# A hand-written order for four engines from the last output tiles to the feed-forward operands, with two inverse norms as powers on GpSimd

## The chip, the cores and the metric

The kernel runs on one core of a Trainium2 chip. Its engines are TensorE (PE; its weight loads are listed apart as PEld), VectorE (DVE), ScalarE (ACT), GpSimd (POOL) and SyncE (SP, which issues the DMAs). The metric is the device time of one execution in microseconds; before the change the median of three runs is 1396.63 us (1396.52 to 1396.65). What a measurement of this kernel can tell from no change is about 0.2%.

## What is computed

One decoder layer on 1024 tokens of width 1024, all in float32: a norm, one input projection, two mixers (sparse attention with 8 heads, and a gated linear recurrence), an output projection added to the residual x, a second norm, and a gated feed-forward of width 2816:

```python
def rms_norm(x, g):
    y = xf * lax.rsqrt(jnp.mean(xf * xf, axis=-1, keepdims=True) + RMS_EPS)
    return (y * g.astype(jnp.float32)).astype(x.dtype)
...
    mix = jnp.concatenate([o_nsa.astype(x.dtype), o_hgrn.astype(x.dtype)], axis=-1)
    x = x + mix @ w_out[l]
    h = rms_norm(x, norm_ffn[l])
    gate, up = jnp.split(h @ w_gate_up[l], 2, axis=-1)
    x = x + (jax.nn.silu(gate) * up) @ w_down[l]
```

The change lies between the last parts of `mix @ w_out` and the first products of `h @ w_gate_up`.

## The kernel before, in words

Every float32 product is made from two parts of each factor, a high part (rounded to the matmul's type fp32r) and the rest. `split` (L111, L112) makes them: ScalarE copies the high part, VectorE subtracts it from the source. `mm3` (L118 to L120) is three matmuls: high by high, high by low, low by high. So the third matmul of a product, in the order of L118, L119, L120 or as the roles fall, needs a part that VectorE wrote.

Tokens are cut into 8 tiles of 128 (t = 0 to 7). For each, attention ends in `out_tile` (24 matmuls in two halves n = 0, 1; VectorE adds each half to x1, L497). Ahead of half 0, `mix_parts` (L510, L511) splits the tile of mixer output. After half 1, `norm_stats` squares the row on ScalarE (L242), and `rsqrt` makes the inverse norm from the sum in 12 VectorE instructions on 128x1 (L125 to L131: three, and three rounds of three). Then for t < 7 ScalarE multiplies x1 by it (L745), and GpSimd by the gain (L746), and subtracts tile t-4 from the first half where t >= 4 (L748). For t = 7 VectorE does both multiplications in one instruction (L743) with a second copy of the gain, g_last, that a DMA brings.

The feed-forward products are made by a two-by-two scheme with seven products per block, in which sums of halves take the place of one product in eight. Its operands are transposed halves of x1 and sums of them: b11 and b21 (tiles 0 to 3), b22 and t1o (tiles 4 to 7), and t2o, t3o, t4o from three differences d per pair of tiles (t, t+4), which GpSimd makes (L987 to L989; the first of pair 3 on VectorE). `operand` (L721 to L728) makes one tile of one operand: four transposes on TensorE into a bank (L724), a copy to the high part on ScalarE (L727), and a subtraction to the low part on VectorE (L728). b11 is ready before the last output tiles. The weights of a product are split like any factor; for the first two column blocks f = 0, 1 the kernel makes two products ahead of the loop: `first[f]` (weights times b11, in banks ps_t) and a second one (weights times b21, L967 sums them). The split weights of `first` lie in the pool `at`; when the block of that pool ends, its memory goes to the pool `ff`, from which the d tiles and the weight pages `epage` come. Then the loop over 22 column blocks begins; its first product is `q = product(s1, t1o)`, whose s1 GpSimd makes from two weight pages (L972).

The order of instructions on each engine is set by a scheduler in the framework, from the code's order and its own costs, except inside blocks that ask for manual scheduling. An engine works through its list in order; an instruction that waits holds up all that stand behind it.

Of the kernel before, what the change touches and what calls it, by code (L numbers as in the profile page):

```python
# [18 lines left out]
P = 128  # L19
# [29 lines left out]
def hybrid_layer(ctx: ExitStack, tc: tile.TileContext, x, x_t, par, w_in, k_norm, pos_k, pos_v,  # L49
# [87 lines left out]
    V.tensor_copy(identb, ident)  # L137
    par_t = const.tile([P, 18], F32, name="par_t")
# [100 lines left out]
    def norm_stats(src, junk):  # L239
# [4 lines left out]
        return rs  # L244

# [484 lines left out]
    with tc.tile_pool(name="at", bufs=1) as at:  # L730
        g_bc = at.tile([P, D], F32, name="g_bc")
        nc.sync.dma_start(g_bc, norm_ffn[0:1, :].broadcast_to([P, D]))
        def nsa_out(t, n):
            if n == 0:
                mixed[t] = mix_parts(qtok[:, t].rearrange("p (c n) -> p c n", c=4))
            out_tile(w_t, t, n, *mixed[t], bank_f)
            if n == 1:
                nc.sync.dma_start(x1_d[t * P:(t + 1) * P, :], x1[:, t, :])
                rs2 = norm_stats(x1[:, t, :], rpage())
                if t == NT - 1:  # L740
                    g_last = rpage()
# [156 lines left out]
        for i, u in enumerate(units + [None]):  # L898
# [46 lines left out]
    single_banks()  # L945
    opA = big.tile([P, 2, 2, 4, 512], F32R, name="opA", tag="A2")
# [3 lines left out]
    b21, t2o, b22, t1o, t3o, t4o = (opA[:, 0], opA[:, 1], opB[:, 0], opB[:, 1], opC[:, 0], opC[:, 1])  # L950
# [3 lines left out]
    def gate_up_a(f):  # L954
# [7 lines left out]
        return a, first.pop(0) if first else product(a[0, 0], b11), product(a[0, 1], b21, o=acc() if f < 2 else None)  # L962
# [335 lines left out]
```

## Time and profile before

| | |
|---|---|
| median of three runs | 1396.63 us |
| profiled execution, own time | 1396.95 us |
| its span, first to last instruction | 1395.2 us |
| TensorE busy | 1366.1 us, 98% of the span |
| VectorE / ScalarE / GpSimd busy | 74% / 43% / 23% |
[...]

The profile is of one execution. Busy time is counted per engine; matmuls overlap in it, so that a row's duration (0.39 us for 128x512) is longer than the step to the next row's start (0.23 us). [...] The stretch of the change lies at about 735 to 790 us of the span.

### The profile page before, as it was taken

To read this page: it belongs to the slowest core of one execution; us is meant where nothing else is said; L and a number is where in the kernel's file an instruction comes from. 1 tells how busy PE (TensorE), PEld (TensorE's weight loads), DVE (VectorE), ACT (ScalarE), POOL (GpSimd) and SP (SyncE) were. 2 spreads that over 40 slices of the span, in tenths; PEclk is the share of its full clock that TensorE was granted. 3 is DMA by queue.
4 is the path that set the end of the run, shared out by engine and by line. 5 is a ranking of instruction groups with operands and counts; after the bars stand their busy time and mean duration, and the time that the engine had idled before them with its cause. 6 is when DMAs were issued, how large, how long until landed. Compare 5 with 4: busy or idle time off the path is not lost.

```text
span 1395.2 us, 19645 instructions
## 1 busy us (share of the span) xinstructions
PE 1366.1 (98%) x7092; PEld 1127.8 (81%) x7092; DVE 1034.3 (74%) x1937; ACT 596.7 (43%) x1153; POOL 322.2 (23%) x297
## 2 busy tenths in 40 slices
PE   9999999999999999999998999999999999999998
PEld 7888888989977777777776788888888888888887
DVE  5317888626688887888867888888888887578764
ACT  7323333323446666566664433333333333444432
POOL 0001111011035443344345533323323320000000
PEclk9999999999999999999999999999999999999999
DMA  8411110111220001000003233333233336998521
GB/s 326 128 46 31 31 31 29 54 31 46 76 106 1 1 1 61 31 16 16 31 17 106 70 112 99 113 114 113 92 113 98 114 98 234 335 327 317 180 94 53
DMA packets 108768, 135.71 MB, mean 97 GB/s; under 512 B 6112, under 2 KB 63872, under 8 KB 108672
## 3 DMA queue, kind: packets, MB, share of 16 engines
q1 hardware_dynamic: 108672, 134.46, 28.6%
q8 instruction: 56, 0.92, 0.3%
q14 instruction: 40, 0.33, 0.1%
HBM read 105.87 MB, written 28.57 MB: 96 GB/s over the span
## 4 chain that ended last, share of the span: by engine, by line
PE 85%; DVE 10%; ACT 2%; issue 1%; POOL 1%; DMA 0%; ACTq 0%; POOLq 0%; DVEq 0%
PE bank L118 9%; PE bank L119 9%; PE bank L120 9%; PE a L118 8%; PE a L120 8%; PE a L119 8%; PE ps_t L120 4%; PE ps_t L119 4%; PE ps_t L118 4%; PE ps_t L861 3%; PE a L865 2%; PE a L866 2%; PE ps_t L375 1%; PE ps_s L839 1%; DVE nm L847 1%
## 5 line engine op out<-in xcount | busy, mean ns | idle before, releaser
L111 ACT ACTIVATE wop<-rpage 128x512 fp32r<-128x512 f32 x132 | 82.7, 630 | 156.8 <-PE bank L120 70.6
L850 POOL TENSOR_SCALAR pbig<-pbig,den,gates 128x640 f32<-128x640 f32 (+7 forms) x128 | 104.0, 817 | 167.0 <-DVE den L849 147.0
L112 DVE TENSOR_TENSOR wop<-rpage,wop 128x512 fp32r<-128x512 f32 x132 | 101.4, 771 | 13.4 <-ACT wop L111 11.3
L864 DVE TENSOR_TENSOR ph<-ps_t,ph 128x512 fp32r<-128x512 f32 x126 | 84.4, 684 | 18.5 <-ACT ph L863 17.6
L863 ACT ACTIVATE ph<-ps_t 128x512 fp32r<-128x512 f32 x126 | 72.7, 595 | 49.6 <-PE ps_t L861 38.7
L861 PE MATMUL ps_t<-ident,pbig 128*128 128x128 f32 x504 | 78.7, 275 | 2.1 <-POOL pbig L850 2.1
L381 POOL TENSOR_TENSOR kp<-kp,fp 128x256 f32<-128x256 f32 x28 | 20.3, 726 | 231.8 <-PE bank L358 180.3
L861 PEld LDWEIGHTS ps_t<-ident,pbig 128*128 128x128 f32 x504 | 61.0, 141 | 11.9 <-POOL pbig L850 3.2
L112 DVE TENSOR_TENSOR wlo<-wraw,whi 128x1024 fp32r<-128x1024 f32 (+2 forms) x27 | 32.0, 1188 | 46.2 <-PE a L120 19.3
L848 ACT ACTIVATE pbig<-ps_s,nm 128x640 f32<-128x640 f32 (+3 forms) x64 | 55.9, 875 | 24.1 <-DVE nm L847 19.0
L118 PE MATMUL bank<-wop 128*128 128x512 f32 x165 | 64.2, 389 | 0.0
L119 PE MATMUL bank<-wop 128*128 128x512 f32 x165 | 64.2, 389 | 0.0
L120 PE MATMUL bank<-wop 128*128 128x512 f32 x165 | 64.2, 389 | 0.0
L1012 POOL TENSOR_TENSOR tmp<-tmp,rpage 128x512 f32<-128x512 f32 x21 | 31.2, 1488 | 139.2 <-DVE wop L112 139.2
L111 ACT ACTIVATE wop<-act_a 128x512 fp32r<-128x512 f32 x48 | 30.3, 631 | 73.8 <-PE bank L120 48.3
L847 DVE TENSOR_REDUCE nm<-ps_s 128x1 f32<-128x640 f32 (+3 forms) x64 | 58.1, 914 | 4.7 <-PE ps_s L842 3.0
L865 PE MATMUL a<-ph,kv 128*128 128x512 f32 x132 | 58.8, 446 | 2.3 <-ACT ph L863 1.6
L866 PE MATMUL a<-ph,kv 128*128 128x512 f32 x132 | 57.5, 435 | 2.9 <-DVE ph L864 2.4
L112 DVE TENSOR_TENSOR wop<-tmp,wop 128x512 fp32r<-128x512 f32 x42 | 43.7, 1039 | 20.6 <-ACT wop L111 19.7
L111 ACT ACTIVATE wop<-tmp 128x512 fp32r<-128x512 f32 x42 | 26.6, 634 | 70.1 <-POOL tmp L1012 37.5
L112 DVE TENSOR_TENSOR wop<-act_a,wop 128x512 fp32r<-128x512 f32 x48 | 33.2, 691 | 30.7 <-ACT wop L111 30.6
L118 PE MATMUL a<-whi,hT_h 128*128 128x256 f32 (+2 forms) x168 | 55.2, 328 | 0.0
(458 smaller groups left out, 4352.3 us busy)
## 6 DMA issues: line engine op xcount, KB each, us to landing
rpage<-in_w_gate_up_dram SPq DMA_DIRECT2D x86, 256.0 KB, 3.1
raws<-in_w_down_dram SPq DMA_DIRECT2D x35, 512.0 KB, 7.5
act_a<-act_d SPq DMA_DIRECT2D x12, 1024.0 KB, 6.1
act_d<-as SPq DMA_DIRECT2D x33, 256.0 KB, 2.2
act_e<-act_d SPq DMA_DIRECT2D x6, 1024.0 KB, 8.2
act_d<-tmp SPq DMA_DIRECT2D x22, 256.0 KB, 2.2
act_d<-th SPq DMA_DIRECT2D x22, 256.0 KB, 2.1
xn<-in_x_dram SPq DMA_DIRECT2D x8, 512.0 KB, 6.0
```

The lines of the kernel that those rows point to most:

```text
L111: A.activation(hi, src, AF.Copy)
L112: V.tensor_tensor(lo, src, hi.bitcast(F32), op=OP.subtract)
L118: PE.matmul(o, ah, bh, start=first, stop=False, skip_group_check=chained)
L119: PE.matmul(o, ah, bl, start=False, stop=False, skip_group_check=chained)
L120: PE.matmul(o, al, bh, start=False, stop=last, skip_group_check=chained)
L847: V.tensor_reduce(nm, sv, axis=AX.XY, op=OP.max, negate=True)
L850: G.tensor_scalar(pp, pp, den, gates[:, qb, h * 3 + 1 + b:h * 3 + 2 + b], op0=OP.mult, op1=OP.mult)
L861: PE.transpose(pt[:, r * P:(r + 1) * P], wts[r][:, c0:c0 + P], ident)
L863: A.activation(ph[:, 0], pt, AF.Copy)
L864: V.tensor_tensor(ph[:, 1], pt, ph[:, 0].bitcast(F32), op=OP.subtract)
L865: PE.matmul(o, vst[b][:, kb, g, :], ph[:, 0], start=b == 0 and kb == kb0, stop=False)
L866: PE.matmul(o, vst[b][:, kb, g, :], ph[:, 1], start=False, stop=False)
```

## The change

Two things are done.

First, for tiles 6 and 7 `norm_power` takes the place of `norm_stats`: ScalarE squares as before, VectorE does one 128x1 multiplication and addition (L253 of the changed kernel), and GpSimd raises the result to the power -0.5 (L256, 128x1, with a constant column mhalf). The 12 small VectorE instructions of each of the two norms go. For tile 7 the power is issued later, where the code says `power()`.

Second, a block of manual scheduling reaches from the first product to the last operands. In it TensorE, VectorE, ScalarE and GpSimd follow the code's order; SyncE's is still the scheduler's. The code is written in a new order: the product first[0], two tiles of b21, the output tile of t = 7 in two different banks, two tiles of b21, first[1]; then for each pair of tiles the operands and differences, with the second product of f = 1 after the operands of pair 0 and that of f = 0 after those of pair 1, where before both came beside the first pairs' operands. The split of the mixer output of tile 7 stands ahead of the out tile; d(3)'s parts are split between VectorE and GpSimd as before. The line numbers grow: L724 to L728 become L743 to L747, L743 becomes L1039, L746 and L748 become L766 and L768, L987 to L989 become L1025, L497 becomes L511, L510 and L511 become L524 and L525.

```diff
+    mhalf = const.tile([P, 1], F32, name="mhalf")
+    V.memset(mhalf, -0.5)
...
+    def norm_power(src, junk):
+
+        ss = small.tile([P, 1], F32, name="n_ss", tag="n_ss")
+        rs = small.tile([P, 1], F32, name="n_rs", tag="n_rs", bufs=NT)
+        A.activation(junk, src, AF.Square, accum_out=ss)
+        V.tensor_scalar(ss, ss, 1.0 / D, EPS, op0=OP.mult, op1=OP.add)
+
+        def power():
+            G.tensor_tensor(rs, ss, mhalf, op=OP.pow)
+            return rs
+        return power
...
-        first = [product(qtok[:, f], b11, at.tile([P, 2, 512], F32R, name="wop0", tag="q", bufs=3), ps_t())
-                 for f in range(2)]
-        for t in nq:
+        hand.enter_context(tc.manual_schedule(engines={mybir.EngineType.PE, mybir.EngineType.DVE,
+                                                       mybir.EngineType.Activation, mybir.EngineType.Pool}))
+        w_first = [at.tile([P, 2, 512], F32R, name="wop0", tag="q", bufs=3) for f in range(2)]
+        for f in range(2):
+            split(w_first[f][:, 0], w_first[f][:, 1], qtok[:, f])
+        for t in nq[:-2]:
             nsa_out(*t)
+        first = [times(w_first[0], b11, ps_t())]
+        mixed[NT - 1] = mix_parts(qtok[:, NT - 1].rearrange("p (c n) -> p c n", c=4))
+        single_banks()
+        opA = big.tile([P, 2, 2, 4, 512], F32R, name="opA", tag="A2")
+        b21, t2o = opA[:, 0], opA[:, 1]
+        for t in range(2):
+            operand(b21, x1[:, t, 512:1024], t, bank_s)
+        nsa_out(*nq[-2])
+        power = nsa_out(*nq[-1], bank_o)
+        for t in range(2, 4):
+            operand(b21, x1[:, t, 512:1024], t, bank_s)
+        first.append(times(w_first[1], b11, ps_t()))
     p12.close()
...
-    nxt = [gate_up_a(0), gate_up_a(1)]
-    for t in range(3):
-        pair_a(t)
-    for t in range(3):
-        pair_d(t)
-        pair_b(t)
-    s1s = [gate_up_s1(0, nxt[0][0])]
+    g_last = rpage()
+    nc.sync.dma_start(g_last, norm_ffn[0:1, :].broadcast_to([P, D]))
+    aw = [gate_up_load(0), gate_up_load(1)]
+    pair_a(0)
+    pair_d(0)
+    pair_d(1, (0, 1))
+    rs2 = power()
+    V.scalar_tensor_tensor(x1[:, NT - 1, :], x1[:, NT - 1, :], rs2, g_last, op0=OP.mult, op1=OP.mult)
+    pair_d(1, (2,))
+    pair_b(0)
+    second = {1: product(aw[1][0, 1], b21, o=acc())}
+    pair_a(1)
+    pair_d(2)
+    pair_b(1)
+    second[0] = product(aw[0][0, 1], b21, o=acc())
+    pair_a(2)
+    V.tensor_tensor(x1[:, 7, 0:512], x1[:, 7, 0:512], x1[:, 3, 0:512], op=OP.subtract)
+    pair_d(3, (0,))
+    pair_b(2)
+    pair_d(3, (1, 2))
+    s1s = [gate_up_s1(0, aw[0])]
     pair_a(3)
-    pair_d(3)
     pair_b(3)
+    hand.close()
```

On TensorE, before, from the last output half (a_7472) to the second products (a_7554 and a_7577, of opA); x and d are sources of transposes:

```order
L119 MATMUL a_7472<-wlo,rpage 128x512
L120 MATMUL a_7472<-whi,rpage 128x512
L724 MATMUL bank<-ident,x_3322 128x128 x32
L724 MATMUL bank<-ident,d_7635 128x128 x4
L724 MATMUL bank<-ident,d_7636 128x128 x4
L724 MATMUL bank<-ident,d_7637 128x128 x4
L724 MATMUL bank<-ident,d_7662 128x128 x4
L724 MATMUL bank<-ident,d_7663 128x128 x3
L118 MATMUL a_7554<-opA,wop 128x512
L119 MATMUL a_7554<-opA,wop 128x512
L118 MATMUL a_7577<-opA,wop 128x512
L119 MATMUL a_7577<-opA,wop 128x512
```

After, from the last matmuls of first[1] (ps_t) to the second product of f = 1 (a_7588), which is now preceded by the 20 transposes of pair 0 alone:

```order
L120 MATMUL ps_t<-b_6855,wop_7392 128x512
L118 MATMUL ps_t<-b_6855,wop_7392 128x512
L119 MATMUL ps_t<-b_6855,wop_7392 128x512
L120 MATMUL ps_t<-b_6855,wop_7392 128x512
L743 MATMUL bank<-ident,x_3324 128x128 x8
L743 MATMUL bank<-ident,d_7553 128x128 x4
L743 MATMUL bank<-ident,d_7555 128x128 x4
L743 MATMUL bank<-ident,d_7557 128x128 x4
L118 MATMUL a_7588<-opA,wop 128x512
L119 MATMUL a_7588<-opA,wop 128x512
L120 MATMUL a_7588<-opA,wop 128x512
L118 MATMUL a_7588<-opA,wop 128x512
```

The first products' last matmuls moved from ahead of the output half to behind it, and one pair's operands stand ahead of a second product where before there were several.

On GpSimd, before, from tile 6's gain (L746) to the weight sum s (L972):

```order
L746 TENSOR_TENSOR x_3322<-x_3322,g_bc 128x1024
L748 TENSOR_TENSOR x_3322<-x_3322 128x512
L987 TENSOR_TENSOR d_7635<-x_3322 128x512
L988 TENSOR_TENSOR d_7636<-d_7635,x_3322 128x512
L989 TENSOR_TENSOR d_7637<-x_3322,d_7635 128x512
L987 TENSOR_TENSOR d_7662<-x_3322 128x512
L988 TENSOR_TENSOR d_7663<-d_7662,x_3322 128x512
L989 TENSOR_TENSOR d_7664<-x_3322,d_7662 128x512
L987 TENSOR_TENSOR d_7689<-x_3322 128x512
L988 TENSOR_TENSOR d_7690<-d_7689,x_3322 128x512
L989 TENSOR_TENSOR d_7691<-x_3322,d_7689 128x512
L972 TENSOR_TENSOR s_7716<-rpage 128x512
```

After, from tile 5's gain (L766) through both powers (L256) to the differences; d_7553 to d_7557 are those of pair 0, d_7559 to d_7565 those of pair 1:

```order
L766 TENSOR_TENSOR x_3324<-x_3324,g_bc 128x1024
L768 TENSOR_TENSOR x_3324<-x_3324 128x512
L256 TENSOR_TENSOR n_rs<-n_ss,mhalf 128x1
L766 TENSOR_TENSOR x_3324<-x_3324,g_bc 128x1024
L768 TENSOR_TENSOR x_3324<-x_3324 128x512
L1025 TENSOR_TENSOR d_7553<-x_3324 128x512
L1025 TENSOR_TENSOR d_7555<-d_7553,x_3324 128x512
L1025 TENSOR_TENSOR d_7557<-x_3324,d_7553 128x512
L1025 TENSOR_TENSOR d_7559<-x_3324 128x512
L1025 TENSOR_TENSOR d_7561<-d_7559,x_3324 128x512
L256 TENSOR_TENSOR n_rs<-n_ss,mhalf 128x1
L1025 TENSOR_TENSOR d_7565<-x_3324,d_7559 128x512
```

The power of tile 7 stands behind five differences that stood behind no power before. Their tiles come from the pool that takes over the memory of `at`.

On VectorE, before, the end of tile 7's inverse norm (L129 to L131) and its multiplication (L743), between evictions of transposes (L728) and weight splits (L112):

```order
L728 TENSOR_TENSOR opB<-bank,opB 128x4x128
L129 TENSOR_TENSOR rs_t<-n_rs 128x1
L728 TENSOR_TENSOR opA<-bank,opA 128x4x128
L130 SCALAR_TENSOR_TENSOR rs_t<-rs_t,rs_v 128x1
L728 TENSOR_TENSOR opC<-bank,opC 128x4x128
L131 SCALAR_TENSOR_TENSOR n_rs<-rs_t,n_rs 128x1
L112 TENSOR_TENSOR wop<-rpage,wop 128x512
L743 SCALAR_TENSOR_TENSOR x_3322<-x_3322,n_rs,rpage 128x1024
L112 TENSOR_TENSOR wop<-epage,wop 128x512
L728 TENSOR_TENSOR opC<-bank,opC 128x4x128
L728 TENSOR_TENSOR opA<-bank,opA 128x4x128
```

After, from the output halves (L511) on, with the multiplication (L1039) ahead of most evictions:

```order
L511 TENSOR_TENSOR x_3324<-a_7456,x_3324 128x512
L511 TENSOR_TENSOR x_3324<-a_7470,x_3324 128x512
L253 TENSOR_SCALAR n_ss<-n_ss 128x1
L747 TENSOR_TENSOR opA<-bank,opA 128x4x128 x2
L747 TENSOR_TENSOR opB<-bank,opB 128x4x128 x2
L1039 SCALAR_TENSOR_TENSOR x_3324<-x_3324,n_rs,rpage 128x1024
L747 TENSOR_TENSOR opA<-bank,opA 128x4x128
L747 TENSOR_TENSOR opC<-bank,opC 128x4x128 x2
L112 TENSOR_TENSOR wop<-epage,wop 128x512
L747 TENSOR_TENSOR opB<-bank,opB 128x4x128 x2
L747 TENSOR_TENSOR opA<-bank,opA 128x4x128
L747 TENSOR_TENSOR opC<-bank,opC 128x4x128 x2
```

The multiplication moved ahead, the small instructions are gone, and the weight splits stand between groups of evictions.

## Rows read from the trace of the kernel before

**Rows 1.** Part 4 of the page: the chain that ended last, share of the span by engine:

```profile
PE 85%; DVE 10%; ACT 2%; issue 1%; POOL 1%; DMA 0%; ACTq 0%; POOLq 0%; DVEq 0%
```

**Rows 2.** Busy time of each engine (instructions) in stretches, granted clock PEclk, DMA share, GB/s:

```profile
749.00:762.00 13.00, 8.46 (x58) 6.11 (x57) 12.14 (x25) 9.53 (x18) 10.67 (x9) 1.00 0.56 161
762.00:774.00 12.00, 9.99 (x58) 7.65 (x58) 10.61 (x15) 5.16 (x11) 7.02 (x6) 1.00 0.15 44
...
786.00:800.00 14.00, 14.00 (x63) 11.58 (x63) 12.15 (x20) 3.70 (x6) 4.46 (x3) 1.00 0.27 83
```

**Rows 3.** TensorE timeline: start us, us, engine line op out<-in xcount:

```profile
739.28 0.39 PE L120 MATMUL ps_t<-b,wop 128*128 128x512 f32 x1
739.51 0.40 PE L118 MATMUL ps_t<-b,wop 128*128 128x512 f32 x1
...
745.07 1.03 PE L724 MATMUL bank<-ident,x 128*128 128x128 f32 x8
746.01 0.50 PE L118 MATMUL a<-whi,rpage 128*128 128x512 f32 x1
```

**Rows 4.** VectorE timeline, same columns; [idle before <-releaser]:

```profile
739.32 0.43 DVE L888 TENSOR_TENSOR qtok<-a,fold 64x256 f32<-64x256 f32 x1
...
739.85 0.42 DVE L510 CAST rpage<-qtok 128x512 fp32r<-128x512 f32 x1
...
746.39 1.29 DVE L728 TENSOR_TENSOR opA<-bank,opA 128x512 fp32r<-128x512 f32 x2 [0.44 <-ACT opA L727]
...
752.26 0.53 DVE L129 TENSOR_TENSOR rs_t<-n_rs 128x1 f32<-128x1 f32 x1
...
761.75 2.30 DVE L743 SCALAR_TENSOR_TENSOR x<-x,n_rs,rpage 128x1024 f32<-128x1024 f32 x1
...
768.98 0.68 DVE L728 TENSOR_TENSOR opA<-bank,opA 128x512 fp32r<-128x512 f32 x1
769.58 1.28 DVE L728 TENSOR_TENSOR opC<-bank,opC 128x512 fp32r<-128x512 f32 x2
...
772.05 0.68 DVE L728 TENSOR_TENSOR opA<-bank,opA 128x512 fp32r<-128x512 f32 x1
```

**Rows 5.** ScalarE timeline of the same stretch:

```profile
738.47 0.38 ACT L886 ACTIVATE fold<-a 64x256 f32<-64x256 f32 x1
741.35 1.15 ACT L745 ACTIVATE x<-x,n_rs 128x1024 f32<-128x1024 f32 x1 [2.49 <-DVE n_rs L131]
745.76 1.09 ACT L727 ACTIVATE opA<-bank 128x512 fp32r<-128x512 f32 x2 [3.26 <-PE bank L724]
```

**Rows 6.** GpSimd timeline of the same stretch:

```profile
742.57 2.41 POOL L746 TENSOR_TENSOR x<-x,g_bc 128x1024 f32<-128x1024 f32 x1 [16.73 <-ACT x L745]
745.06 1.28 POOL L748 TENSOR_TENSOR x<-x 128x512 f32<-128x512 f32 x1
746.29 1.30 POOL L987 TENSOR_TENSOR d<-x 128x512 f32<-128x512 f32 x1
...
761.29 1.69 POOL L973 TENSOR_TENSOR rpage<-rpage 128x512 f32<-128x512 f32 x1
```

**Rows 7.** GpSimd timeline, 780 to 785 us:

```profile
781.91 1.63 POOL L1015 TENSOR_TENSOR epage<-epage,tmp 128x512 f32<-128x512 f32 x1
```

**Rows 8.** VectorE timeline, 780 to 784 us:

```profile
782.53 1.55 DVE L112 TENSOR_TENSOR wop<-tmp,wop 128x512 fp32r<-128x512 f32 x1 [0.15 <-ACT wop L111]
```

**Rows 9.** TensorE timeline, 766 to 778 us:

```profile
773.68 0.48 PE L118 MATMUL bank<-opB,wop 128*128 128x512 f32 x1
...
774.23 0.39 PE L120 MATMUL bank<-opB,wop 128*128 128x512 f32 x1
```

**Rows 10.** Busy time and granted clock in four stretches around 424 us:

```profile
421.00:424.00 3.00, 1.35 (x10) 0.88 (x8) 2.18 (x7) 2.62 (x9) 3.00 (x5) 1.00 0.00 0
424.00:427.00 3.00, 3.00 (x15) 2.52 (x14) 2.96 (x10) 1.97 (x7) 1.93 (x4) 0.54 0.01 3
```

**Rows 11.** The same view, 751 to 757.8 us:

```profile
751.00:754.40 3.40, 1.86 (x12) 1.20 (x12) 3.16 (x8) 2.88 (x8) 2.93 (x3) 1.00 0.92 260
```

More of the change, by code (lines that the diff above doesn't have):

```diff
@@ L714, in product, with times @@
         split(w[:, 0], w[:, 1], src)
+        return times(w, op, o)
+    def times(w, op, o):
         for c in range(4):
@@ L961, in gate_up_a @@
                 gu_load(a[k, j], FS[f], j, k)
-        return a, first.pop(0) if first else product(a[0, 0], b11), product(a[0, 1], b21, o=acc() if f < 2 else None)
+        return a
+    def gate_up_a(f):
+        a = gate_up_load(f)
+        return a, product(a[0, 0], b11), product(a[0, 1], b21)
     def gate_up_sum(f, o1, o2):
@@ L979, in pair_a, with pair_d @@
         operand(b22, x1[:, t + 4, 512:1024], t, bank_s)
-        if t == 3:
-            V.tensor_tensor(x1[:, 7, 0:512], x1[:, 7, 0:512], x1[:, 3, 0:512], op=OP.subtract)
         operand(t1o, x1[:, t + 4, 0:512], t, bank_s)
-    def pair_d(t):
+    def pair_d(t, some=(0, 1, 2)):
         xa, xb = x1[:, t, :], x1[:, t + 4, :]
-        d = dif[t] = [ff.tile([P, 512], F32, name=f"d{i}", tag="d", bufs=6) for i in range(3)]
-        (G if t < 3 else V).tensor_tensor(d[0], xb[:, 512:1024], xb[:, 0:512], op=OP.subtract)
-        G.tensor_tensor(d[1], d[0], xa[:, 0:512], op=OP.subtract)
-        G.tensor_tensor(d[2], xa[:, 512:1024], d[0], op=OP.subtract)
+        for i in some:
+            d = ff.tile([P, 512], F32, name=f"d{i}", tag="d", bufs=6)
+            dif[t, i] = d
+            (G if t < 3 or i else V).tensor_tensor(d, *((xb[:, 512:1024], xb[:, 0:512]), (dif[t, 0], xa[:, 0:512]),
+                                                       (xa[:, 512:1024], dif[t, 0]))[i], op=OP.subtract)
     def pair_b(t):
         for i, op in enumerate((t2o, t3o, t4o)):
-            operand(op, dif[t][i], t, bank_s)
-    for t in range(4):
-        operand(b21, x1[:, t, 512:1024], t, bank_s)
-    nxt = [gate_up_a(0), gate_up_a(1)]
-    for t in range(3):
-        pair_a(t)
-    for t in range(3):
-        pair_d(t)
-        pair_b(t)
-    s1s = [gate_up_s1(0, nxt[0][0])]
+            operand(op, dif[t, i], t, bank_s)
+    g_last = rpage()
[4 more added lines that the diff above has]
+    pair_d(1, (0, 1))
+    rs2 = power()
+    V.scalar_tensor_tensor(x1[:, NT - 1, :], x1[:, NT - 1, :], rs2, g_last, op0=OP.mult, op1=OP.mult)
[12 more added lines that the diff above has]
+    s1s = [gate_up_s1(0, aw[0])]
     pair_a(3)
-    pair_d(3)
     pair_b(3)
+    hand.close()
+    nxt = [(aw[f], first[f], second[f]) for f in range(2)]
     tmp = big.tile([P, 16, 512], F32, name="tmp", tag="A1")
```

25 lines of the change are left out of this document (12 added, 13 removed).

## The prediction

> **What bounds the kernel now.** I read the page's chain first, then the busy times of the changed stretch by stage, then each engine's timeline there. By the chain TensorE sets 85% of the span and VectorE 10% [rows 1], so a change pays only where TensorE idles. In the stretch it idles in one place. From 749 to 774 us it is busy 18.45 of 25 us, while VectorE is busy 22.75 [rows 2]: the evictions of transposes pace it, one per 0.60 us (768.98 to 769.58, [rows 4]). Idle time there, 6.55 us, is all that any order of this stage can win. After it TensorE has no slack, 14.00 of 14.00 us [rows 2], so what is late when the loop's first product q starts (773.68, [rows 9]) stays late to the end.
>
> **Part 1, the powers.** VectorE loses twelve 128x1 instructions per tile. For tile 7, nine of them lie between 752.26 and 761.75 with nine 0.60 us instructions of other kinds [rows 4]: 9.49 - 5.40 = 4.1 us of VectorE's time, the bounding engine's. That is the gain on offer. In exchange GpSimd gets a 128x1 power twice. No row shows one. From its 128x1024 (2.41) and 128x512 (1.28) operations [rows 6] a zero-column one costs 1.28 - 1.13 = 0.15 us; a dear one may cost as much as a whole 1024-column one, 2.41. I take 0.3, near the small end, as only one column is worked on, and keep both ends.
>
> **Part 2, the order up to the end of first[1].** First[0] ends where the next product starts now, 739.51 [rows 3]. Eight transposes take 745.07 to 746.01, 0.94 us [rows 3]: 740.45. Then the output half wants the low part of the mixer tile at its third matmul, at about 740.9. VectorE ends the second fold at 739.32 + 0.43 and a cast of 0.42 [rows 4], so it could subtract (L525) from 740.2. But GpSimd's gain of tile 6 (2.41 us, [rows 6]) is ready at about 740.1: ScalarE's fold ends at 738.85 and its scaling takes 1.15 [rows 5], the first power having been done by then. When VectorE's two-input subtraction from SBUF meets a GpSimd operation the rows show it waiting: L112 at 782.53 lasted 1.55 [rows 8], where an undisturbed subtraction of its size takes 0.68 (768.98, [rows 4]), and ended at 784.08, 0.54 after GpSimd's operation did (781.91 + 1.63, [rows 7]). So L525 ends at 740.07 + 2.41 + 0.54 = 743.0, and TensorE's third matmul starts at 743.1: 2.2 us lost. If VectorE is first, GpSimd is late by about 0.4 and these 2.2 us are not lost.
>
> [...]
>
> From there: 22 matmuls at 0.23 (739.28 to 739.51, [rows 3]) make 748.2, eight transposes 749.1, first[1]'s 12 matmuls 751.9.
>
> **Part 3, the wait that is new.** The first difference of pair 0 takes memory that pool `at` gives back, and the last reader of that memory is first[1]. Before, both first products were over when GpSimd came to it; now first[1] ends at 751.9. So GpSimd, free after L766 and L768 at about 743.8, waits 8 us. Behind it stand four more differences and the power of tile 7: 752.0 + 5 x 1.28 [rows 6] + 0.3 = 758.7. Behind the power VectorE's multiplication L1039 waits, and GpSimd has the next difference running by then. The same pair cost 2.30 us before: L743 started 0.46 after L973 and ended 1.07 after it (761.75 + 2.30 against 761.29 + 1.69, [rows 4, 6]). So L1039 ends at 761.0. VectorE works in order; three evictions of pair 0 stand behind (1.8): 762.8, then the split L112 of the second product's weights, 0.68 and some 0.15 of handover: its third matmul starts at 763.6. In that time TensorE, which has finished pair 0's transposes by about 758, has nothing that it may do: 5.5 us idle. The saved 4.1 us fall into this wait and buy nothing.
>
> **Part 4, groups and products in turn.** After this TensorE and VectorE alternate. Ten matmuls left of the second product: 765.9. The first eviction ends no sooner than 1.32 us after its group's first transpose starts, its subtraction starting then (745.07 to 746.39, [rows 3, 4]): 767.2. Five evictions 3.0, split and handover 0.83: 771.1. Ten matmuls: 773.4. The last group: 1.32, ten evictions and two subtractions at 0.60, 7.2, and about 1.1 where VectorE waits for two extra copies on ScalarE (0.54 each by [rows 5]): 783.0. With the handover q starts at 783.2, against 773.68: 9.5 us late. Before, q's third matmul came 0.55 after its first, without a wait [rows 9]. Now its split stands behind the two sums of the first products on VectorE: 0.6 x 3 less two matmuls, 1.4; the next product's split is late by about 1.3 in the same way. Sum 12.2.
>
> **Part 5, the clock.** Where TensorE was busy 1.35 of 3.00 us, the next 3 us ran at a granted clock of 0.54, the lower level; where it was busy 1.86 of 3.40, nothing fell [rows 10, 11]. The waits of 743 (2.2 us), 758 to 763.6 and those of the groups leave such thin stretches two or three times. A low stretch of 3 us costs between nothing, if TensorE waits in it anyway, and 1.4 us (0.46 x 3); I take 2 in all, of 0 to 5.
>
> The sum is 12.2 + 2 = 14.2 on the profiled execution's 1396.95 us (span 1395.2), which is 0.3 above the median of the three runs: 1396.63 + 14.2 = 1410.8, rounded to 1411.
>
> **Rivals.**
>
> *The differences don't wait* (0.13). If the memory isn't the one I think, GpSimd has the power of tile 7 done at about 750.5, and L1039 waits for nothing but its turn: after first[1], 751.9 + 1.32 and two evictions, at 754.4. It ends at 755.5, three evictions 757.3, split 758.1, and the rest as above: 760.4, 765.5, 767.8, 777.4, q at 777.7, 4.0 late, and 2.7 more at q: 6.7, or 4.5 without the wait at 743. 1401 to 1404. For it: the order of the pools is the framework's. Against it: nothing in the trace, since before the first difference started right behind L748, at 746.29 [rows 6], when first[1] had long ended.
>
> *A dear power and a low clock* (0.11). At 2.41 us each, the first power is hidden behind GpSimd's 8 us of waiting, the second is not: 2.1 more. If the clock stays at its lower level from 752 to 783, the two times ten matmuls on the path take 0.2 us more each, 4 in all, the transposes ahead of each group's first eviction some 0.5 each: 5.5 in the place of 2. Together 12.2 + 2.1 + 5.5 = 19.8, 1416; without the 2.1, 1414. For it: no power is in the trace, and three waits follow one another. Against it: one column is worked on, and evictions set the groups' time at either level.
>
> [...]
>
> *VectorE's freed time reaches TensorE, faster* (0.05). This is decided at one point: is the power of tile 7 done before VectorE comes to L1039 at 754.4, that is, does GpSimd start the first difference by 754.4 - 0.3 - 6.4 = 747.7? If so and if TensorE's products cover the evictions between them, VectorE starts on its backlog at 748.8 and needs the 23.7 us of before (749.07 to 772.73, [rows 4]) less 4.1 and less 1.2 of L743's wait: 767.2, q at 768.2, 5.5 earlier: 1391. Against it: TensorE has ten matmuls and the 1.32 us between two groups in which VectorE has nothing to do, twice 3.6 us, which alone eats the gain.
>
> *No change* (0.05): half of the faster case with the groups' waits, within 0.2% (2.8 us, what a measurement of this kernel can tell), 1394 to 1399.
>
> **How the numbers follow.** The forecast has 0.66, with its own range of 1405 to 1416: the sum without the wait at 743 and without the clock is 1396.6 + 10 = 1406.6, with the wait and the clock's upper end 1414, and a power of 2.41 us adds 2.1. The range for 8 times in 10 reaches to the first rival below and half of the second above: 1401 to 1418. Faster by over 0.2%: 0.05. Within: 0.05. Slower: 0.66 + 0.13 + 0.11 = 0.90.
>
> **What would show it.** In the trace of the changed kernel: L1025's first instruction on GpSimd starts right behind the last matmul of first[1], at about 752, with an idle time of some 8 us before it; L1039 waits for the power L256, and VectorE idles about 4 us before it; TensorE idles 5 us before the second product's third matmul, released by L112; L525 lasts 2.5 instead of 0.7 us; q starts near 783; behind q the two kernels' instructions run at one distance. The stage's VectorE time without idling falls by 4 us. I am wrong if the first difference starts near 744, or if TensorE is busy more than 20 of the 25 us between 749 and 774.

## The result, and the profile after

The changed kernel takes 1413.47 us (median of four runs, 1412.47 to 1414.38), the kernel before 1396.64: a ratio of 1.0121, with an interval of 1.0101 to 1.0141. A fourth execution of the kernel before took 1502.94 us and is left out of the ratio. 1411 was forecast. The profiled execution took 1414.38 us, its span is 1412.6. The granted clock is the share of full speed that the profile gives TensorE in a stretch; its mean over the span is 0.990 here and 0.997 in the kernel before. The lowest value in any window read here is 0.50 (743 to 746 us, below); "the low clock" means that.

Executions do not reach the stage of the change at one time. The second fold of the last attention block (L888, now L908) starts at 739.32 in the trace of before [rows 4] and at 737.74 here, though no instruction was moved ahead of tile 6's norm (the last section says why). So **lateness** below is counted from that row to the span's end: 1412.6 - 737.74 against 1395.2 - 739.32, which is 19.0 us. 1.58 us added to a time of this trace gives the time on the axis of the prediction.

The three stretches of [rows 2], in the changed kernel (window, length, then busy time of TensorE, its weight loads, VectorE, ScalarE, GpSimd, then granted clock, DMA share, GB/s):

```profile
749.00:762.00 13.00, 7.17 (x37) 4.90 (x35) 5.75 (x9) 5.63 (x10) 9.68 (x8) 0.79 0.62 182
762.00:774.00 12.00, 8.31 (x32) 6.39 (x32) 5.79 (x10) 3.22 (x6) 3.48 (x3) 0.66 0.23 66
...
786.00:800.00 14.00, 11.81 (x40) 9.25 (x41) 12.41 (x16) 7.36 (x13) 8.25 (x7) 0.76 0.27 76
```

From 749 to 774 TensorE is busy 15.48 us instead of 18.45, at clocks of 0.79 and 0.66, and VectorE, which was busy 22.75, only 11.54: the stage is no longer paced by evictions, every engine waits. GpSimd's timeline, the counterpart of [rows 6]:

```profile
735.96 0.56 POOL L256 TENSOR_TENSOR n_rs<-n_ss,mhalf 128x1 f32<-128x1 f32 x1 [11.66 <-DVE n_ss L253]
738.53 2.36 POOL L766 TENSOR_TENSOR x<-x,g_bc 128x1024 f32<-128x1024 f32 x1 [2.00 <-ACT x L765]
...
752.17 1.27 POOL L1025 TENSOR_TENSOR d<-x 128x512 f32<-128x512 f32 x1 [9.59 <-DVE opA L747]
...
757.31 1.26 POOL L1025 TENSOR_TENSOR d<-d,x 128x512 f32<-128x512 f32 x1
758.53 0.56 POOL L256 TENSOR_TENSOR n_rs<-n_ss,mhalf 128x1 f32<-128x1 f32 x1
759.05 1.27 POOL L1025 TENSOR_TENSOR d<-x,d 128x512 f32<-128x512 f32 x1
760.28 2.25 POOL L1025 TENSOR_TENSOR d<-x 128x512 f32<-128x512 f32 x1
```

The first difference starts at 752.17, 0.25 us after TensorE went on from first[1], behind 9.59 us of idle time, and the power of tile 7 comes at 758.53, right behind the five differences that stand ahead of it on GpSimd, though VectorE wrote its input (L253) from 750.35 to 750.50. (The releaser named, an eviction on VectorE, is not the last one: that eviction ended at about 742.7. In the trace of e1, below, the releaser named is first[1] itself.) A power of 128x1 took 0.56 us, the first as the second. VectorE's timeline, the counterpart of [rows 4]:

```profile
738.66 2.77 DVE L525 TENSOR_TENSOR rpage<-qtok,rpage 128x512 fp32r<-128x512 f32 x1
...
759.12 2.28 DVE L1039 SCALAR_TENSOR_TENSOR x<-x,n_rs,rpage 128x1024 f32<-128x1024 f32 x1 [4.65 <-POOL n_rs L256]
...
763.12 1.30 DVE L112 TENSOR_TENSOR wop<-epage,wop 128x512 fp32r<-128x512 f32 x1
770.64 1.32 DVE L747 TENSOR_TENSOR opB<-bank,opB 128x512 fp32r<-128x512 f32 x2 [6.21 <-ACT opB L746]
```

L525 lasts 2.77 us beside GpSimd's L766; the multiplication L1039 waits 4.65 us for the power, and takes 2.28 us, as L743 did (2.30, [rows 4]); between the groups VectorE is idle 6.21 us. TensorE's timeline, the counterpart of [rows 3, 9]:

```profile
741.49 0.50 PE L120 MATMUL a<-whi,rpage 128*128 128x512 f32 x1 [2.05 <-DVE rpage L525]
...
751.69 0.39 PE L120 MATMUL ps_t<-b,wop 128*128 128x512 f32 x1
751.92 1.03 PE L743 MATMUL bank<-ident,x 128*128 128x128 f32 x8
...
759.76 0.80 PE L118 MATMUL a<-opA,wop 128*128 128x512 f32 x1 [3.02 <-ACT wop L111]
...
764.48 0.79 PE L120 MATMUL a<-opA,wop 128*128 128x512 f32 x1 [3.49 <-DVE wop L112]
765.07 0.63 PE L118 MATMUL a<-opA,wop 128*128 128x512 f32 x1
765.50 0.63 PE L119 MATMUL a<-opA,wop 128*128 128x512 f32 x1
...
786.55 0.50 PE L118 MATMUL bank<-opB,wop 128*128 128x512 f32 x1 [2.44 <-ACT wop L111]
...
788.92 0.80 PE L120 MATMUL bank<-opB,wop 128*128 128x512 f32 x1 [1.64 <-DVE wop L112]
```

The brackets give the length of a wait and what ended it. The clock between some of these rows, the same columns as above:

```profile
743.00:746.00 3.00, 3.00 (x8) 2.34 (x7) 0.69 (x1) 0.00 (x0) 0.00 (x0) 0.50 0.02 5
...
764.00:769.00 5.00, 4.52 (x11) 3.45 (x12) 0.42 (x1) 0.00 (x0) 1.56 (x1) 0.50 0.28 83
771.00:776.00 5.00, 3.43 (x18) 2.29 (x17) 3.34 (x6) 2.25 (x5) 0.00 (x0) 1.00 0.00 0
...
789.00:794.00 5.00, 5.00 (x12) 3.94 (x13) 4.85 (x6) 2.82 (x5) 3.22 (x2) 0.50 0.00 0
```

From 735 to 800 us TensorE's waits, by the view of waits, sum to 17.5 us; in the kernel before they sum to 6.4. The difference of 11.1 and the low clock on the path (6.2, worked out in "The size") make 17.3 of the 19.0; the rest is not assigned. At the low clock matmuls stepped by 0.43 us (765.07 to 765.50) instead of 0.23 ([rows 3]).

### The profile page after: what moved, and what is told of

It reads as the page before. It is cut to its first block, busy times and chain, and to the rows that moved or that the text cites. A ratio compares the mean times of both kernels' runs of the same rounds, so it can differ in the third digit from the quotient of the medians.

```text
span 1412.6 us, 19630 instructions
## 1 busy us (share of the span) xinstructions
PE 1372.4 (97%) x7092; PEld 1131.6 (80%) x7092; DVE 1035.5 (73%) x1916; ACT 597.3 (42%) x1153; POOL 324.9 (23%) x299
## 4 chain that ended last, share of the span: by engine, by line
PE 84%; DVE 10%; ACT 3%; issue 1%; POOL 1%; DMA 0%; ACTq 0%; POOLq 0%; DVEq 0%
PE bank L120 9%; PE bank L118 9%; PE bank L119 9%; PE a L120 8%; PE a L119 8%; PE a L118 8%; PE ps_t L118 4%; PE ps_t L119 4%; PE ps_t L120 4%; PE ps_t L881 3%; PE a L885 2%; PE a L886 2%; PE ps_t L389 1%; PE ps_s L859 1%; DVE nm L867 1%
## 5 line engine op out<-in xcount | busy, mean ns | idle before, releaser
L112 DVE TENSOR_TENSOR wop<-rpage,wop 128x512 fp32r<-128x512 f32 x132 | 102.4, 777 | 13.3 <-ACT wop L111 11.2
L112 DVE TENSOR_TENSOR wlo<-wraw,whi 128x1024 fp32r<-128x1024 f32 (+2 forms) x27 | 32.0, 1188 | 46.0 <-PE a L120 19.3
L112 DVE TENSOR_TENSOR wop<-act_a,wop 128x512 fp32r<-128x512 f32 x48 | 33.2, 691 | 33.8 <-ACT wop L111 33.7
L112 DVE TENSOR_TENSOR wop<-tmp,wop 128x512 fp32r<-128x512 f32 x42 | 42.7, 1018 | 18.6 <-ACT wop L111 18.0
```

Of the source, the lines that this page charges most:

```text
L112: V.tensor_tensor(lo, src, hi.bitcast(F32), op=OP.subtract)
```

## The experiments

Every run is compared with the kernel before on the same chip; "late" is the lateness defined above, from the run's profiled execution. It is one execution's, with that execution's low clock in it; what a run won or lost is read from the medians. The intervals of e1, e5 and e6 overlap that of the changed kernel, those of e3 and e7 just touch it, the others lie clear of it.

| run | median us | ratio to before (95%) | late us |
|---|---|---|---|
| changed kernel | 1413.47 | 1.0121 (1.0101 to 1.0141) | 19.0 |
| e1 power early | 1410.84 | 1.0104 (1.0089 to 1.0119) | 13.0 |
| e2 first[1] in front | 1407.56 | 1.0080 (1.0065 to 1.0095) | 12.3 |
| e3 by hand, no powers | 1408.95 | 1.0089 (1.0074 to 1.0104) | 13.1 |
| e4 powers alone | 1401.50 | 1.0034 (1.0024 to 1.0045) | 4.7 |
| e5 added matmuls | 1412.37 | 1.0112 (1.0098 to 1.0126) | 16.0 |
| e6 mix first | 1411.23 | 1.0104 (1.0090 to 1.0118) | 15.6 |
| e7 s early | 1409.36 | 1.0088 (1.0075 to 1.0102) | 12.5 |
| e8 reordered | 1397.44 | 1.0005 (0.9996 to 1.0014) | 1.3 |
| e9 e2 and e7 | 1404.96 | 1.0060 (1.0045 to 1.0075) | 8.6 |
| e10 no order by hand | 1402.78 | 1.0045 (1.0032 to 1.0059) | 5.4 |
| e11 multiplication first | 1396.69 | 1.0004 (0.9995 to 1.0013) | -0.5 |
| e12 e11 without powers | 1397.41 | 1.0006 (0.9997 to 1.0015) | 1.3 |

**e1, the power of tile 7 ahead of the differences.**

```diff
     pair_a(0)
+    rs2 = power()
     pair_d(0)
     pair_d(1, (0, 1))
-    rs2 = power()
```

> One move: the power of tile 7 stands on GpSimd ahead of the differences of pair 0 instead of behind five of them. Theory A (the power is late because it stands behind differences that wait for the memory of first[1], and VectorE's multiplication waits for it): the power is done near 751, the multiplication starts after two evictions of opB at about 754.5 instead of 759.1, and the second product's third matmul comes 3.5 to 4.5 us earlier, limited next by the split of its weight page, whose copy waits for a DMA that landed at 759.1; 1407 to 1410. Rival B (the alternation of groups and products sets the time, whatever the power does): not below 1412. Rival C (the two powers themselves are dear): no change.

Measured 2.6 us less than the changed kernel, 1410.84, just above theory A's range; the intervals of the two ratios overlap, so the mechanism is read from the trace. GpSimd, VectorE and ScalarE of e1:

```profile
752.84 1.27 POOL L1025 TENSOR_TENSOR d<-x 128x512 f32<-128x512 f32 x1 [1.02 <-PE ps_t L120]
```

```profile
755.46 2.30 DVE L1039 SCALAR_TENSOR_TENSOR x<-x,n_rs,rpage 128x1024 f32<-128x1024 f32 x1 [0.31 <-POOL d L1025]
...
760.49 1.51 DVE L112 TENSOR_TENSOR wop<-epage,wop 128x512 fp32r<-128x512 f32 x1 [0.94 <-ACT wop L111]
```

```profile
759.83 0.63 ACT L111 ACTIVATE wop<-epage 128x512 fp32r<-128x512 f32 x1 [1.81 <-DMA epage<-in_w_gate_up_dram]
```

The difference still waits, and what ends its wait is first[1] (ps_t). The multiplication no longer waits for a power, only 0.31 us until a difference is over. The next bound is as expected the split's copy, which waits for a DMA: the page's memory, too, comes from the pool that first[1] reads, and in the changed kernel its DMA is issued at 752.68, 0.76 us after TensorE went on from first[1] (751.92); in the kernel before, with first[1] in front, the first of the two was issued at 745.01. So the power's place was one wait of two; the other one has the same cause. The lateness in this trace fell by 6.0 us, more than the median: 1.6 of them are a low clock behind the wait for L525 that did not come here, though nothing was changed there (last section).

**e2, first[1] ahead of the output halves.**

```diff
-        first = [times(w_first[0], b11, ps_t())]
+        first = [times(w_first[f], b11, ps_t()) for f in range(2)]
...
-        first.append(times(w_first[1], b11, ps_t()))
```

> One move: the product first[1] stands on TensorE directly behind first[0], ahead of the output halves of tile 7, as in the kernel before; the rest of the order by hand stays. Theory A: its 12 matmuls fill the 2.05 us in which TensorE waits for L525, the differences and the weight pages no longer wait for it, the power of tile 7 is done when VectorE comes to it, and pair 0 starts 3.9 us earlier; second product's third matmul near 756.5 instead of 764.5; with less low clock 1403 to 1406. Rival B (groups and products in turn): only the 2 us of L525 are won, 1411 to 1412. Rival D (the memory wait is not first[1]'s): differences start at 752 again, 1411.

Measured 1407.56, 5.9 us less, above theory A's range and far from its rivals' 1411. GpSimd and VectorE:

```profile
742.90 1.29 POOL L1024 TENSOR_TENSOR d<-x 128x512 f32<-128x512 f32 x1
...
749.74 0.56 POOL L256 TENSOR_TENSOR n_rs<-n_ss,mhalf 128x1 f32<-128x1 f32 x1 [0.34 <-DVE n_ss L253]
```

```profile
753.90 1.30 DVE L1038 SCALAR_TENSOR_TENSOR x<-x,n_rs,rpage 128x1024 f32<-128x1024 f32 x1 [1.42 <-DMA rpage<-in_norm_ffn_dram]
```

The first difference starts at 742.90 instead of 752.17, without idle time, and the power at 749.74: what held both was first[1], as the prediction said. The gain fell short of the forecast. Its trace shows another wait, 1.42 us for the DMA of g_last, and the low clock, which was expected to shrink, in three places again (steps of 0.43 us at 758 to 760, 767 to 770 and 783 to 788); how much each of them cost is not shown.

**e3, the order by hand without the powers.**

```diff
-                if t < NT - 2:
-                    rs2 = norm_stats(x1[:, t, :], rpage())
-                else:
-                    power = norm_power(x1[:, t, :], rpage())
-                    if t == NT - 1:
-                        return power
-                    rs2 = power()
+                rs2 = norm_stats(x1[:, t, :], rpage())
+                if t == NT - 1:
+                    return rs2
```

> The order by hand stays, the two powers go back to twelve small VectorE instructions each. Theory A (what the power saved falls into a wait): VectorE makes tile 7's inverse norm itself by about 752.7, the multiplication waits for nothing at 755 to 756, so this kernel is faster than the changed one in spite of some 5 us more VectorE work: 1406 to 1411. Rival E (the power saves VectorE time that counts, and the order alone is the loss): 1415 to 1418.

1408.95, as theory A says: with more work on VectorE the kernel is 4.5 us faster than the changed one. In its trace tile 7's multiplication (L1034 there) starts at 755.10 without a wait, while the first difference still waits for first[1], until 751.31. Two things are mixed in it: tile 7's norm no longer waits for GpSimd, and tile 6's comes later, so that L525 meets no GpSimd operation (0.69 us in its trace), which e6 prices alone.

**e4, the powers alone**, in the kernel before with the scheduler's order.

```diff
-                rs2 = norm_stats(x1[:, t, :], rpage())
+                rs2 = (norm_stats if t < NT - 2 else norm_power)(x1[:, t, :], rpage())
```

> The kernel before with the two powers alone, all engines ordered by the scheduler. The nine to twelve small VectorE instructions go from a stage that VectorE paces, 4 us. Theory F (freed VectorE time reaches TensorE when no order by hand stands against it): 1392 to 1394. Theory G (the scheduler's list shifts with it, and what is won ahead of q is given back where q's split stands): 1395 to 1400. Rival C (powers are dear): above 1400.

1401.50, some 5 us slower than before: theory F is wrong, and the time lies above what G gave and in the range of C. The trace tells C from G. TensorE and VectorE around q:

```profile
773.72 0.50 PE L118 MATMUL bank<-opB,wop 128*128 128x512 f32 x1
...
777.64 0.50 PE L120 MATMUL bank<-opB,wop 128*128 128x512 f32 x1 [3.19 <-DVE wop L112]
...
781.64 0.50 PE L120 MATMUL bank<-opA,wop 128*128 128x512 f32 x1 [0.85 <-DVE wop L112]
```

```profile
775.71 1.28 DVE L979 TENSOR_TENSOR tmp<-a,tmp 128x512 f32<-128x512 f32 x2
776.90 0.68 DVE L112 TENSOR_TENSOR wop<-s,wop 128x512 fp32r<-128x512 f32 x1
```

The powers take 0.56 us here too, and tile 7's multiplication waits for a DMA (1.15 us), not for the power. q starts as late as before (34.1 us behind the second fold; before 773.68 - 739.32 = 34.4), but its third matmul waits 3.19 us for a split that the scheduler now puts behind two sums of the first products, and the next product 0.85. That is theory G with its size underrated: the time that was freed ahead of q was lost again at q.

**e5, matmuls added in two waits.**

```diff
+    def warm(n):
+        o = bank_s()
+        for i in range(n):
+            PE.matmul(o, b11[:, 0, 0, 0:P], b11[:, 0, 0], start=i == 0, stop=i == n - 1)
...
+    warm(30)
     second = {1: product(aw[1][0, 1], b21, o=acc())}
...
     pair_b(3)
+    warm(16)
     hand.close()
```

> The changed kernel, and in two of TensorE's waits matmuls that nobody reads: 30 of 128x512 ahead of the second product of f = 1 (from 756.7 to about 763.6, where the product's third matmul came at 764.5) and 16 ahead of q (783 to 786.7). They take no work away. Theory K (the low clock behind thin stretches costs on the path): matmuls at 764 to 769 and at 789 to 794 step 0.23 instead of 0.43 us, ten and some ten of them, 2.0 + 2.2 us less: 1408.5 to 1411. Rival (the clock falls in time that is waited anyway, or for another reason): within 1 us of the changed kernel, 1412.5 to 1414.5; if the added matmuls get in the way, later.

1412.37: 1.1 us less, between the two ranges; inconclusive by time. The clock in e5:

```profile
764.00:768.00 4.00, 4.00 (x23) 3.37 (x22) 0.24 (x1) 0.05 (x1) 1.40 (x1) 1.00 0.31 87
...
771.00:776.00 5.00, 4.41 (x11) 3.23 (x12) 1.27 (x3) 0.20 (x1) 0.00 (x0) 0.67 0.00 0
...
788.00:793.00 5.00, 3.63 (x14) 2.54 (x15) 4.85 (x6) 2.81 (x6) 3.29 (x2) 1.00 0.00 0
```

In both places the product ran at full clock (1.00 in the first and the third row), as theory K says; but now the clock fell to 0.67 at 771 to 776, over the other second product, which ran at full clock in the changed kernel (1.00 for the same window, above). The third low stretch, behind L525, is missing in e5 as well (1.00 from 744 to 747 us), though nothing was changed there. So the low clock can be taken away at one place and come at another; that it would go if the waits went is not shown by this run.

**e6, VectorE ahead of GpSimd at L525.** The scaling of tile 6 is issued after two operand tiles.

```diff
-                    rs2 = power()
-                A.activation(x1[:, t, :], x1[:, t, :], AF.Copy, scale=rs2)
...
+                    rs2 = power()
+                    if hand_on:
+                        return lambda: scale(t, rs2)
+                scale(t, rs2)
...
         for t in range(2):
             operand(b21, x1[:, t, 512:1024], t, bank_s)
+        scale6[-1]()
         nsa_out(*nq[-2])
```

> The changed kernel with ScalarE's scaling of tile 6, and GpSimd's two operations behind it, moved behind two evictions in the code, so that VectorE's L525 (738.7) starts ahead of GpSimd's L766 (then about 740.8). Theory L (L525 loses 2.05 us because GpSimd's operation started first): L525 lasts 0.7 us, TensorE's output half waits for nothing, and the low clock at 743 to 746 (1.4 us) goes with the wait; GpSimd's later end is hidden by its wait for first[1]. 2 to 3.5 us less: 1410 to 1411.5. Rival (L525 waits for something else, or GpSimd's delay counts): no change, 1413 to 1414.5.

1411.23, 2.2 us less, in theory L's range. L525 in e6:

```profile
738.66 0.69 DVE L525 TENSOR_TENSOR rpage<-qtok,rpage 128x512 fp32r<-128x512 f32 x1
```

It starts at the same 738.66 and takes 0.69 us instead of 2.77. By time alone e6 and the changed kernel overlap; the row does not. In e6 GpSimd's operation starts only at 740.82, when L525 is over, so this run prices the meeting and does not show who wins one. The changed kernel's rows show both orders: L525, 0.13 us behind L766, lasts until 0.5 us after it; and the difference that GpSimd starts at 760.28, while VectorE's L1039 runs, takes 2.25 us instead of 1.27. The kernel before has the second order too: L973, which started at 761.29, 0.15 us behind L112 on VectorE, took 1.69 us [rows 6], where L987, on operands of the same size, took 1.30: 0.4 late, as part 2 has it for this order.

```profile
761.14 0.68 DVE L112 TENSOR_TENSOR wop<-rpage,wop 128x512 fp32r<-128x512 f32 x1
```

In these three meetings the one that started second took longer than undisturbed; why is not shown.

**e7, the weight sum s and q's split earlier.**

```diff
+    s1s = [gate_up_s1(0, aw[0])]
+    w_s.append(wring.tile([P, 2, 512], F32R, name="wop", tag="w"))
+    split(w_s[0][:, 0], w_s[0][:, 1], s1s[0])
     pair_a(2)
...
-    s1s = [gate_up_s1(0, aw[0])]
     pair_a(3)
...
-        q = product(s1, t1o)
+        q = times(w_s.pop(), t1o, bank8()) if w_s else product(s1, t1o)
```

> The changed kernel with the weight sum s on GpSimd and q's split moved ahead of the operands of pair 2; GpSimd idled there from 765.6 to 780.9. Theory Q (q's start and its third matmul wait, 2.44 and 1.64 us, because s and its split stand behind the last differences and VectorE's two sums): both waits go, and with them the low clock at 789 to 794; 4 to 6 us less, 1407.5 to 1409.5. Rival (the next split waits in its place): 0 to 2 us less, 1411.5 to 1413.5.

1409.36, 4.1 us less, as theory Q says. q's first and third matmul, 0.54 us apart as in [rows 9] (0.55), and no low clock behind them (1.00 in every window from 786 to 801 us):

```profile
785.31 0.48 PE L118 MATMUL bank<-opB,wop 128*128 128x512 f32 x1
...
785.85 0.40 PE L120 MATMUL bank<-opB,wop 128*128 128x512 f32 x1
```

**e8, an order that follows from this.** A summary of its core in the code's order, not the diff itself (pair_a, pair_d, pair_b as in the change):

```text
first[0]; b21 of tiles 0, 1; first[1]; output halves 0, 1; b21 of tiles 2, 3
pair_d(0); pair_a(0); pair_a(1); power; split f=1; pair_b(0); pair_d(1); second[1]
split f=0; multiplication of tile 7; pair_a(2); s; pair_b(1); second[0]; split of s
pair_d(2); subtraction; pair_d(3, (0,)); pair_b(2); pair_d(3, (1, 2)); pair_a(3); pair_b(3); sums; end of the block
```

> An order by hand that follows from the theory, with the powers: both first products ahead of pair 0's differences (first[0], two tiles of b21, first[1], the two output halves, two tiles of b21), the power of tile 7 ahead of the differences of pair 1, four operand tiles ahead of each second product, their splits and q's split ahead of the evictions that stood before them, the manual block up to VectorE's two sums. Theory A with Q (the order's waits are the loss and the 4 us of VectorE's small instructions are to be had): VectorE's backlog from 749 is 4 us shorter than in the kernel before, q starts 2 to 4 us earlier; some of it lost at the loop's next splits: 1393 to 1396. Rival B (the alternation of groups and products costs whatever the order): 1399 to 1404.

1397.44: 16 us faster than the changed kernel with the same powers and the same kind of block, so rival B is out; but above theory A's range and no faster than before (interval 0.9996 to 1.0014), so the 4 us were not had. q starts where it started before (34.4 us behind the second fold in both). Three of VectorE's instructions that met GpSimd's:

```profile
758.52 2.29 DVE L1046 SCALAR_TENSOR_TENSOR x<-x,n_rs,rpage 128x1024 f32<-128x1024 f32 x1
...
765.04 1.75 DVE L1054 TENSOR_TENSOR x<-x 128x512 f32<-128x512 f32 x1
766.83 1.65 DVE L1025 TENSOR_TENSOR d<-x 128x512 f32<-128x512 f32 x1
```

Against 1.07 (what L743 took behind GpSimd's end, [rows 4, 6]) and two times 0.68 they lost 3.3 us, GpSimd at work beside each. The first took as long in the kernel before (2.30); the other two meetings, 2.0 us, are new.

**e9, e2 and e7 together.** Beside the two diffs it has a third change: the second output half of tile 7 stands behind the b21 operands of tiles 2 and 3.

> The two moves of e2 and e7 together in the changed kernel: first[1] ahead of the output halves, the weight sum s and q's split ahead of pair 2. Measured apart they took 5.9 and 4.1 us off 1413.5. Theory (two places, each with its own wait and the low clock behind it): they add up, 1402 to 1405. Rival (one wait that the other move also shortens, VectorE's evictions): 1405.5 to 1407.5.

1404.96: 8.5 us less than the changed kernel, where 5.9 and 4.1 sum to 10; at the upper end of the theory's range. Both moves pay; because of the third change the difference to 10 is not read as an overlap of the two.

**e10, the changed code without its block of manual scheduling.**

```diff
-        hand.enter_context(tc.manual_schedule(engines={mybir.EngineType.PE, mybir.EngineType.DVE,
-                                                       mybir.EngineType.Activation, mybir.EngineType.Pool}))
```

> The changed kernel's code without the block of manual scheduling: same code, same powers, the scheduler orders all engines. Theory R (the loss is in the order by hand, not in the code's new arrangement or the powers): near the kernel with the powers alone (1401.5): 1399 to 1403. Rival (the new arrangement of products and operands in the code carries the loss): 1407 to 1414.

1402.78, theory R: of the 16.8 us, 10.7 go with the order by hand; what stays is about what the powers alone cost under the scheduler (e4).

**e11, tile 7's multiplication ahead of a split.**

```diff
-    split(w_sec[0][:, 0], w_sec[0][:, 1], aw[0][0, 1])
     V.scalar_tensor_tensor(x1[:, NT - 1, :], x1[:, NT - 1, :], rs2, g_last, op0=OP.mult, op1=OP.mult)
+    split(w_sec[0][:, 0], w_sec[0][:, 1], aw[0][0, 1])
```

> e8 with one move: tile 7's multiplication ahead of the split of the second product of f = 0, where VectorE waited 0.97 us for that split's copy and GpSimd idled 3.5 us for a DMA; in e8 it started 0.4 us after GpSimd's sum s and took 2.29 instead of 1.07 us. Theory S (what the powers save is eaten by two-input VectorE instructions that meet GpSimd's): the instruction takes 1.1, VectorE's backlog is some 2 us shorter, 1394.5 to 1396.5. Rival (the next collision takes its place): 1397 to 1399.

1396.69, between the two ranges, and the same as before. The multiplication took 1.27 us (theory S said 1.1), and q came 1.0 us earlier than before (33.4 us behind the second fold against 34.4); the time does not show it.

```profile
757.35 1.27 DVE L1045 SCALAR_TENSOR_TENSOR x<-x,n_rs,rpage 128x1024 f32<-128x1024 f32 x1
```

**e12, e11's order with the powers taken back.** The diff of e3 on e11.

> e11's order, with the two powers back as twelve small VectorE instructions each. Theory V (a power takes 4.1 us off VectorE's backlog, as the prediction counted from the rows of before): 1400 to 1401.5. Theory W (most of those 4.1 us were waits of small two-input instructions behind GpSimd's operations, and undisturbed twelve of them take 2.3 us): tile 7's norm is made in 2.3 us, perhaps beside one or two of GpSimd's differences, 1397.5 to 1399.5. Rival (nothing depends on it): 1396 to 1397.

1397.41, between W's range and the rival's, and not to be told from e11 (the intervals overlap), though in the two traces q starts 1.8 us later behind the second fold here; theory V is out. Three of the nine small instructions that follow the first three of tile 7's norm:

```profile
750.39 0.71 DVE L129 TENSOR_TENSOR rs_t<-n_rs 128x1 f32<-128x1 f32 x1
751.13 1.19 DVE L130 SCALAR_TENSOR_TENSOR rs_t<-rs_t,rs_v 128x1 f32<-128x1 f32 x1
752.36 0.16 DVE L131 SCALAR_TENSOR_TENSOR n_rs<-rs_t,n_rs 128x1 f32<-128x1 f32 x1
```

Two of them met GpSimd's differences (0.71 and 1.19 us, each ending 0.02 us after the difference it met), seven took 0.16.

## Why the prediction was right

**The sign and the mechanism.** The wait of part 3 is there link by link: difference at 752.17 behind first[1]; power behind five differences; L1039 behind the power; its end at 761.40 (762.98 on the prediction's axis, 761.0 forecast). e2 moved the cause and the chain went with it; e1 cut one link of it, and its trace names first[1] as what ends the wait. The rival in which the differences do not wait is excluded by both. The 2.2 us at L525 (part 2) are 2.05, and in e6, where GpSimd's operation comes later, they are gone (0.69 instead of 2.77). The meeting comes with tile 6's power, which makes GpSimd's operation ready early (it starts at 740.11 on the prediction's axis, before at 742.57): in every run with the powers but e6 this subtraction takes 2.8 us, in those without (before, e3, e12) 0.69. TensorE's waits behind pair 0, at the groups and at q's third matmul stand where they were forecast, the last larger (1.64 for 1.4); the one at the product after q (1.3) did not come. e7 shows the one at q alone.

**The size.** The steps ran, on the prediction's axis: out half's third matmul 743.07 (743.1 forecast), first[1]'s end 753.5 (751.9), second product's third matmul 766.06 (763.6), its end 770.5 (765.9), q 788.13 (783.2). Most of what they were off came from the clock. Part 5 put it at 2 us in all, of 0 to 5, and that was the term with the wrong size: in this execution it is 6.2. By the starts in the trace, ten steps from 742.52 to 746.40 took 3.88 us instead of 2.30 (1.6 late), ten of the second product from 764.48 to 768.91 took 4.43 (2.1), and twelve behind q from 788.92 to 794.17 took 5.25 instead of 2.76 (2.5), a place that the sum did not count. With 6.2 in the place of 2 the sum of 14.2 gives 18.4, against a lateness of 19.0. The last 0.6 is a difference: up to q the other steps took 1.2 us more than forecast (among them the power, 0.56 instead of 0.3, and the split L112, 1.30 instead of 0.68), behind q they took 0.6 less.

This agreement holds for one execution, the slowest of the four; in the medians the kernel is 16.8 slower. The clock term is not the same in every execution: the stretch of 1.6 is missing in e1, e5 and e7, which have the same wait ahead of it (2.05, 2.05 and 2.04 us). So how near 1411 comes to the median is in part luck. e5 does not prove the term by time: two low stretches went with the added matmuls, a new one came, and it won 1.1 us.

**A step that was wrong without harm.** Part 1 took 4.1 us of VectorE's time as the gain on offer. e12 shows that they are not a property of the twelve instructions: undisturbed the small two-input ones took 0.16 us there, 0.19 from one start to the next. By the same reading the one of 0.53 us in [rows 4], like L743 with 2.30 (1.27 in e11), was waiting for GpSimd: it ended at 752.79, and the difference beside it at 752.78.

```profile
751.51 1.27 POOL L988 TENSOR_TENSOR d<-d,x 128x512 f32<-128x512 f32 x1
```

With the small ones gone, other two-input instructions met GpSimd in their place: L525 with 2.8 us, and two more in e8 (1.75 and 1.65 us, where 0.68 is undisturbed). So the rival in which freed time makes the kernel faster promised too much with its 1391: with a better order (e11) the whole is the same as before. That the meetings alone eat the gain is a reading of these rows; no run takes them all away.

**Left open.** What the stage would take with no low clock at all, and what the low clock costs in an execution other than the profiled one; and whether an order exists that keeps VectorE's two-input instructions out of GpSimd's way throughout, which e11 did at one place only.

## What to carry to other kernels

When a block of code is put into a fixed order, follow for each engine what its first blocked instruction holds up behind it; here a buffer's last reader, moved behind other work, held a queue of five, a power (it started at 758.53, in e2 at 749.74), and with it the engine that paced the stage. An instruction's cost read from a trace can include its wait for another engine (here L525's 2.77 us were 0.69 in e6): check how long the same instruction takes undisturbed before counting its removal as a gain. And look past the end of the stage: e4 lost its time, and e7 won its own, at the first product behind it, by where one split stood.

## What the runs showed of the hardware that was not expected

The same wait can be followed by the low clock in one execution and not in another. About 421 to 424 us, far ahead of the change, TensorE is busy 1.35 of 3.00 us in the kernel before, and the next 3 us run at 0.54 [rows 10]. The changed kernel has the same stretch:

```profile
421.00:424.00 3.00, 1.36 (x11) 0.94 (x10) 2.18 (x9) 2.62 (x9) 3.00 (x4) 1.00 0.00 0
424.00:427.00 3.00, 3.00 (x22) 2.61 (x21) 2.99 (x9) 1.98 (x7) 2.31 (x5) 1.00 0.01 3
```

1.36 us busy, and then full clock, with 22 instructions in the 3 us in place of 15. An estimate from the granted clock is 0.46 x 3 = 1.4 us, most of the 1.58 us by which this execution reached the stage earlier. It is not the order of the instructions that decides: in e5, where as far as the traces show they stand there in the same order as in the changed kernel, TensorE is busy 1.38 us and the clock falls to 0.58:

```profile
424.00:427.00 3.00, 3.00 (x17) 2.58 (x16) 2.99 (x9) 1.97 (x7) 2.30 (x5) 0.58 0.01 3
```

The wait for L525 shows the same. Behind it the changed kernel ran at 0.50 (743 to 746, above); e1, as long after the same wait, at full clock:

```profile
743.79 0.50 PE L120 MATMUL a<-whi,rpage 128*128 128x512 f32 x1 [2.05 <-DVE rpage L525]
```

```profile
745.30:748.30 3.00, 3.00 (x15) 2.49 (x14) 0.69 (x1) 0.00 (x0) 0.00 (x0) 1.00 0.02 5
```

So in these traces the busy share does not tell whether the clock falls behind it, and the argument of part 5 (1.35 of 3.00 fell, 1.86 of 3.40 did not) was weaker than it looked.
